# A gated decoder block on one core: the ring of split weights becomes pages, and more of the weight sums are formed by transfers

## The chip, the core and the metric

The kernel runs on one core of a Trainium2 chip. The metric is device time in microseconds (us). TensorE multiplies (PE; its weight loads are listed apart as PEld), VectorE (DVE) and ScalarE (ACT) work on tiles in on-chip memory, GpSimd (POOL) and SyncE (SP) issue transfers here. Transfers from both queues run on the same 16 DMA engines.

## The reference

One decoder block on 256 tokens of width 4096, all in float32:

```
h = rmsnorm(x, norm_w)
u_p, z_p, u_c, b_c, c_c, z_c, g = split(h @ w_in)           # w_in: 4096 x 20480
y_pool = pool(u_p) @ pool_w * pool_scale * silu(z_p)         # trailing means over 2, 4, 8, 16 tokens
y_conv = b_c * conv3(c_c * u_c) * silu(z_c)                  # causal, width 3
br     = [y_pool @ w_branch[0], y_conv @ w_branch[1]]        # 2048 x 4096 each
x      = x + sum(sigmoid(g + gate_b) * br) @ w_out           # 4096 x 4096
out    = rmsnorm(x, final_norm_w)
```

Nearly all the arithmetic is in products of 256 tokens with w_in, w_branch and w_out.

## The kernel before

**Units and steps.** The output columns are cut into 32 units of 1024 columns: convolution units (cu0, cc0, cz0, cb0, cu1, ...), pool units (pz0, pu0, pz1, pu1), gate units (g0_0, g1_0, g0_1, ... g1_3), branch units (b0_0 ... b1_3) and output units (o0 ... o3). A unit runs over its rows in steps of 256 rows. A step loads one raw block of weights (1 MB, 128 partitions x 2 x 1024) into one of three raw buffers.

**Splitting.** A float32 value is multiplied as a high part and a low part. ScalarE writes the high part of a block into the ring (`act`), VectorE writes the remainder, raw minus high (`sub`), and TensorE then multiplies high x high, high x low and low x high, three matmuls of 128 x 512 for each block product.

**Two kinds of step.** A P step makes plain products: 24 matmuls, two VectorE subtractions of 128 x 1024. An S step is one level of a Strassen-like scheme: 21 matmuls instead of 24, but sums of weight blocks are to be formed first. Its raw block has four quarters q0 to q3. Two first sums v = (q0 + q1, q0 + q2) and two last sums (v0 + q2, that + q3) are formed in float32, and then q1, q2, q3, the two v and the two last sums are split. In the code these are `sums` (v into tile V, one VectorE addition of 128 x 1024), `direct` (splits q1 to q3, forms the last sums in tile W), `t13` (splits v) and `t24` (splits W). A table PLACES says which steps of each unit are S steps; there are 207 of them.

**Helped steps.** For some S steps v is not formed by VectorE. SyncE loads q0 twice into a free half of tile E (512 KB), then GpSimd issues a transfer that adds q1 and q2 to it from memory (512 KB). Tile E holds two such halves (`sums_in`, `place_of_sum`); they are free between the end of the last unit's epilogue (`e_done`) and the unit's end. Table HELPED lists which S steps of a unit may be helped, and the rule in `pump` takes one when a half is free and the step's own raw load is at most three loads ahead (LEAD). 53 of the 207 steps are helped.

**The ring.** Split parts lie in a ring of 62 KB a partition, cut into contiguous pieces (`Ring.alloc`): 16 KB for a P step, 28 KB for an S step. Pieces are released in order as matmul groups finish.

**What sets the order.** The program is written out ahead by a planner in Python. `run_step` emits the matmul groups of a step; after every few groups `pump` emits what can be prepared now: a raw load if its buffer has been split (`split`), a sum load, and the splitting of steps up to three ahead, if the ring has room. Every six matmuls `tick` advances a counter `now`, emits one item of the queued epilogue of the unit before, and one item of `fills`. Fills prepare the left operands of the branch and output units: `Fill.fetch` loads 256 KB into a stage (sa, sb or a part of Y), by GpSimd's queue, and ScalarE and VectorE split it into the operand region. All engines then run their lists in order. A raw buffer is released when `direct` has run, so the next load may start while `t13` and `t24` are still to come.

Line numbers of the profile: L69 is `act`, L72 the VectorE helper of all additions and subtractions, L87 SyncE's loads, L91 GpSimd's moves, L94 GpSimd's adding transfers, L1292 the matmul.

Of the kernel before, what the change touches and what calls it, by code (L numbers as in the profile page):

```python
# [32 lines left out]
P = 128  # L33
T = 256
# [11 lines left out]
RING = 62  # L46
# [5 lines left out]
PACE = 5  # L52
TAIL = 3
# [3 lines left out]
def hybrid_block(ctx: ExitStack, tc: tile.TileContext, x, x_t, norm_t, w_first, w_in, pool_w, pool_scale,  # L57
# [48 lines left out]
    ring = sb("ring", [P, RING * KB], F32R)  # L106
# [4 lines left out]
    W = sb("W", [P, 2, NH])  # L111
# [93 lines left out]
    class Ring:  # L205


        def __init__(self, size):
            self.size, self.head, self.live = size, 0, []

        def alloc(self, n):
            at = self.head if self.head + n <= self.size else 0
            for a, m, _, _ in self.live:
                if at < a + m and a < at + n:
                    return None
            if at == 0 and self.head + n > self.size and any(a >= self.head for a, *_ in self.live):
                return None
            block = [at, n, 0, n]
            self.live.append(block)
            self.head = at + n  # L220
            return block

        def release(self, block, n):
            block[2] += n
            while self.live and self.live[0][2]:
                first = self.live[0]
                first[0] += first[2]
                first[1] -= first[2]
                first[2] = 0
                if first[1]:  # L230
                    break
                self.live.pop(0)

    rg = Ring(RING)

    def piece(block, off, n):
        o = (block[0] + off) * KB
        return ring[:, o:o + n * KB]


# [5 lines left out]
    class Step:  # L246
# [7 lines left out]
        def micros(self):  # L254
# [3 lines left out]
            def half(n):  # L258
                def f(block):
                    self.blocks[n] = block  # L260
                    self.h[n] = piece(block, 0, 4).rearrange("p (k n) -> p k n", k=2)
                    self.l[n] = piece(block, 4, 4).rearrange("p (k n) -> p k n", k=2)
                    q = r.rearrange("p (k n) -> p k n", k=2)[:, :, n * NH:(n + 1) * NH]
                    if self is steps[0] and n == 0:

                        act(self.h[n][:, 0], q[:, 0])
                        x_direct(0)
                        for k in range(2):
                            if k:
                                act(self.h[n][:, k], q[:, k])  # L270
                            sub(self.l[n][:, k], q[:, k], self.h[n][:, k].bitcast(F32))
                        return
                    if self is steps[0]:
                        for k in range(2):
                            act(self.h[n][:, k], q[:, k])
                            sub(self.l[n][:, k], q[:, k], self.h[n][:, k].bitcast(F32))
                        return
                    act(self.h[n], q)
                    sub(self.l[n], q, self.h[n].bitcast(F32))
                return f  # L280

            if self.kind == "P":
                self.blocks, self.h, self.l = [None] * 2, [None] * 2, [None] * 2
                return self.pre + [(8, None, half(0)), (8, None, half(1))] + self.post
            if self.kind == "S":
# [8 lines left out]
                def direct(block):  # L294
                    self.bd = block
                    d = piece(block, 0, 12).rearrange("p (i a n) -> p i a n", i=3, a=2)
                    self.dh, self.dl = d[:, :, 0], d[:, :, 1]
                    act(self.dh, q[:, 1:4])
                    add(W[:, 0], v[:, 0], q[:, 2])
                    sub(self.dl, q[:, 1:4], self.dh.bitcast(F32))  # L300
                    add(W[:, 1], W[:, 0], q[:, 3])
                    self.split = True

                def t13(block):
                    self.b13 = block
                    t = piece(block, 0, 8).rearrange("p (i a n) -> p i a n", i=2, a=2)
                    self.h13, self.l13 = t[:, :, 0], t[:, :, 1]
                    act(self.h13, v)
                    sub(self.l13, v, self.h13.bitcast(F32))
                    self.summed = True  # L310

                def t24(block):
                    self.b24 = block
                    t = piece(block, 0, 8).rearrange("p (i a n) -> p i a n", i=2, a=2)
                    self.h24, self.l24 = t[:, :, 0], t[:, :, 1]
                    act(self.h24, W)
                    sub(self.l24, W, self.h24.bitcast(F32))

                return self.pre + self.post + ([] if helped else [(0, None, sums)]) + [(12, lambda: not helped or self.added, direct), (8, None, t13), (8, None, t24)]
            if self.kind == "B":  # L320
                def parts(block):
                    self.block = block
                    self.h = piece(block, 0, 8).rearrange("p (t n) -> p t n", t=2)
                    self.l = piece(block, 8, 8).rearrange("p (t n) -> p t n", t=2)
                    act(self.h, R)
                    sub(self.l, R, self.h.bitcast(F32))

                return [(16, lambda: self.unit.flags.get("base"), parts)]
            if self.kind == "M":
                g = self.g  # L330
                e = E.rearrange("p a n -> p (a n)")[:, g * 1024:(g + 1) * 1024].rearrange(
                    "p (k t) -> p k t", k=4)

                def weights(block):
                    self.bw = block
                    self.h = piece(block, 0, 8).rearrange("p (k n) -> p k n", k=4)
                    self.l = piece(block, 8, 8).rearrange("p (k n) -> p k n", k=4)
                    q = r.rearrange("p (k n) -> p k n", k=4)
                    act(self.h, q)
                    sub(self.l, q, self.h.bitcast(F32))  # L340

                def pooled(block):
                    self.ba = block
                    self.ah = piece(block, 0, 4).rearrange("p (k t) -> p k t", k=4)
                    self.al = piece(block, 4, 4).rearrange("p (k t) -> p k t", k=4)
                    act(self.ah, e)
                    sub(self.al, e, self.ah.bitcast(F32))

                return [(16, None, weights), (8, lambda: self.unit.flags.get(f"pooled{g}"), pooled)]

        def groups(self):

            gs = []
            if self in steps[0:2]:

                for n in range(2):
# [3 lines left out]
                    for i, k in order:  # L360
                        for t in range(2):
                            ah, al = self.op.standing(k, t)
                            h, l = self.h[n][:, k], self.l[n][:, k]
                            gs.append([("E", t, n), [((ah, h), (al, h), (ah, l))[i]], None])
                    gs[-1][2] = [(self.blocks[n], 8)]
            elif self.kind == "P":
                order = [(t, n) for n in self.halves for t in self.toks]
                if self.ending or self.opening:
                    order = [(t, n) for t in self.toks for n in self.halves]
                for t, n in order:  # L370
                    mm = []
                    for k in range(2):
                        ah, al = self.op.standing(k, t)
                        h, l = self.h[n][:, k], self.l[n][:, k]
                        mm += [(ah, h), (ah, l), (al, h)]
                    gs.append([("E", t, n), mm, None])
                    if self.final and t == self.toks[-1]:
                        gs[-1][2] = [(self.blocks[n], 8)]
            elif self.kind == "S":
                prods = {"M1": (A11, self.dh, self.dl, 0, ("F", 0, 0)),  # L380
                         "N3": (Q3, self.dh, self.dl, 1, ("E", 0, 0)),
                         "M2": (A12, self.dh, self.dl, 2, ("E", 0, 1)),
# [1202 lines left out]
```

## Time and profile before

| | before |
|---|---|
| median of 3 runs | 2375.21 us (2372.78 to 2377.42) |
| span of the profiled execution | 2371.9 us |
| granted TensorE clock over the span | 0.999 |
| moved by DMA | 605.60 MB, mean 255 GB/s |

The profile gives no time of the profiled execution beside its span, which runs from the first to the last instruction; the span lies 3.3 us below the median of the runs and 0.9 us below the fastest, so some 1 to 5 us of a run lie around it. An engine's busy time is the union of its instructions; matmuls overlap each other, so the 390 ns of one matmul is longer than the time from one to the next.

### The profile page before, as it was taken

Reading aid. Unit: us, or ns where it says so; the run is one execution under the profiler, and the core shown is the slowest. Engines: PE = TensorE matmul, PEld = TensorE weight load, DVE = VectorE, ACT = ScalarE, POOL = GpSimd, SP = SyncE. Lnnn points to the kernel's source line nnn. Section 1 sums busy time; section 2 is a strip of 40 time slices with the busy share of each in tenths; the row PEclk is TensorE's granted clock in tenths of the full one; section 3 lists DMA queues with packets and bytes.
Section 4 is the critical chain, followed back from the end, with each engine's and each line's share of the span. In section 5 each row is a group of like instructions: output and inputs, shape, how many; then the busy total and the mean of one; then the engine's idle time right before and its main releaser. Section 6 shows DMA issues by size and latency. Waiting matters only on the chain.

```text
span 2371.9 us, 28071 instructions
## 1 busy us (share of the span) xinstructions
PE 2353.5 (99%) x10483; PEld 1946.2 (82%) x10483; DVE 2176.7 (92%) x2234; ACT 1419.7 (60%) x1474; POOL 134.5 (6%) x201
## 2 busy tenths in 40 slices
PE   9999999999999999999999999999999999999998
PEld 7888888888888888888888888887878888878886
DVE  8999899989999989989999999988998898899898
ACT  7565565656555656566665656565664556566564
POOL 0000000000002001000000000001100001000000
PEclk9999999999999999999999999999999999999999
DMA  8578678886778658658887888789866667778867
GB/s 335 189 253 252 224 263 276 261 253 215 262 252 265 224 211 251 231 219 262 278 281 232 295 285 276 244 285 293 285 240 226 260 229 267 244 241 285 280 222 267
DMA packets 105257, 605.60 MB, mean 255 GB/s; under 512 B 11232, under 2 KB 11488, under 8 KB 43936
## 3 DMA queue, kind: packets, MB, share of 16 engines
q1 hardware_dynamic: 83216, 512.30, 59.5%
q0 software_dynamic: 21472, 90.45, 16.0%
q8 instruction: 82, 1.34, 0.2%
q10 hardware_dynamic: 432, 1.07, 0.1%
q14 instruction: 55, 0.45, 0.1%
HBM read 571.26 MB, written 25.17 MB: 251 GB/s over the span
## 4 chain that ended last, share of the span: by engine, by line
PE 90%; DVE 5%; DMA 2%; issue 2%; ACT 1%; SPq 0%; POOL 0%; DVEq 0%; ACTq 0%; POOLq 0%
PE sums L1292 66%; PE shared L1292 22%; DVE ring L72 2%; PE shared L804 1%; PE shared L528 1%; DVE W L72 1%; ACT ring L69 1%; DMA R<-in_gate_b_dram 1%; DMA E<-in_w_in_dram 1%; DVE R L72 0%; DMA raw<-in_w_in_dram 0%; DVE V L72 0%; DVE arena L72 0%; DMA raw<-in_w_out_dram 0%; DVE sa L72 0%
## 5 line engine op out<-in xcount | busy, mean ns | idle before, releaser
L1292 PE MATMUL sums<-ring,arena 128*128 128x512 f32 x7641 | 1806.5, 390 | 2.8 <-ACT E L69 2.4
L1292 PEld LDWEIGHTS sums<-ring,arena 128*128 128x128 f32 x7641 | 1431.6, 188 | 301.1 <-ACT E L69 3.3
L72 DVE TENSOR_TENSOR ring<-raw,ring 128x1024 fp32r<-128x1024 f32 (+2 forms) x695 | 942.4, 1382 | 101.8 <-ACT ring L69 97.7
L69 ACT ACTIVATE ring<-raw 128x1024 fp32r<-128x1024 f32 (+2 forms) x695 | 801.8, 1182 | 284.9 <-PE sums L1292 174.9
L1292 PE MATMUL shared<-ring,arena 128*128 128x512 f32 x2484 | 627.7, 389 | 3.6 <-DVE ring L72 3.6
L1292 PEld LDWEIGHTS shared<-ring,arena 128*128 128x128 f32 x2484 | 465.5, 188 | 102.9 <-DVE ring L72 6.0
L69 ACT ACTIVATE ring<-W 128x1024 fp32r<-128x1024 f32 x207 | 219.9, 1062 | 364.2 <-DVE W L72 302.9
L72 DVE TENSOR_TENSOR ring<-W,ring 128x1024 fp32r<-128x1024 f32 x207 | 253.9, 1226 | 23.1 <-ACT ring L69 11.8
L69 ACT ACTIVATE ring<-V 128x1024 fp32r<-128x1024 f32 x154 | 162.7, 1057 | 144.5 <-DVE V L72 119.9
L72 DVE TENSOR_TENSOR V<-raw 128x1024 f32<-128x1024 f32 x154 | 187.9, 1220 | 7.6 <-DMA raw<-in_w_in_dram 6.8
L72 DVE TENSOR_TENSOR ring<-V,ring 128x1024 fp32r<-128x1024 f32 x154 | 187.9, 1220 | 1.3 <-ACT ring L69 1.3
L72 DVE TENSOR_TENSOR W<-W,raw 128x512 f32<-128x512 f32 x207 | 141.9, 685 | 0.0
L72 DVE TENSOR_TENSOR W<-V,raw 128x512 f32<-128x512 f32 x154 | 106.6, 692 | 4.7
L94 POOL DMA_DIRECT2D E<-in_w_in_dram x47 | 41.1, 875 | 765.1 <-DMA E<-in_w_in_dram 322.7
L72 DVE TENSOR_TENSOR R<-R,E 128x1024 f32<-128x1024 f32 (+1 forms) x49 | 77.1, 1592 | 4.0 <-DMA R<-in_gate_b_dram 1.8
L72 DVE TENSOR_TENSOR ring<-E,ring 128x1024 fp32r<-128x1024 f32 x57 | 69.5, 1219 | 1.9 <-ACT ring L69 1.9
L69 ACT ACTIVATE ring<-E 128x1024 fp32r<-128x1024 f32 x57 | 59.7, 1047 | 6.7 <-PE sums L1292 3.7
L72 DVE TENSOR_TENSOR R<-R,shared 128x512 f32<-128x512 f32 x87 | 59.6, 685 | 2.7 <-ACT R L69 0.8
L69 ACT ACTIVATE arena<-sa 128x512 fp32r<-128x512 f32 (+2 forms) x48 | 25.2, 555 | 57.5 <-DVE sa L72 57.5
L69 ACT ACTIVATE E<-sums,rin 128x512 f32<-128x512 f32 x76 | 49.2, 682 | 15.7 <-PE sums L1292 15.7
L72 DVE TENSOR_TENSOR W<-E,raw 128x512 f32<-128x512 f32 x53 | 36.6, 691 | 12.8 <-issue 5.7
L72 DVE TENSOR_TENSOR arena<-sa,arena 128x512 fp32r<-128x512 f32 (+2 forms) x48 | 27.5, 600 | 3.5 <-ACT arena L69 3.5
(143 smaller groups left out, 560.0 us busy)
## 6 DMA issues: line engine op xcount, KB each, us to landing
raw<-in_w_in_dram SPq DMA_DIRECT2D x318, 1024.0 KB, 5.5
raw<-in_w_branch_dram SPq DMA_DIRECT2D x64, 1024.0 KB, 5.2
raw<-in_w_out_dram SPq DMA_DIRECT2D x64, 1024.0 KB, 5.9
E<-in_w_in_dram SPq DMA_DIRECT2D x47, 512.0 KB, 7.3
E<-in_w_in_dram POOLq DMA_DIRECT2D x47, 512.0 KB, 8.6
gates_d<-R POOLq DMA_DIRECT2D x8, 1024.0 KB, 12.0
R<-in_gate_b_dram POOLq DMA_DIRECT2D x7, 1024.0 KB, 12.0
R<-E POOLq DMA_DIRECT2D x4, 1024.0 KB, 9.4
```

What stands on the lines that cost most here:

```text
L69: return pin(nc.scalar.activation(dst, src, func, **kw))
L72: return pin(nc.vector.tensor_tensor(out=dst, in0=a, in1=b, op=op))
L94: return pin(nc.gpsimd.dma_start(dst, src, accum_op=ALU.add))
L528: pin(nc.tensor.transpose(shared(j)[:, i * T + t * P:i * T + (t + 1) * P], src[:, t, c:c + P], ident))
L804: pin(nc.tensor.matmul(o, a[:, k, ts], b[:, k], start=(k, i) == (0, 0), stop=(k, i) == (3, 2)))
L1292: pin(nc.tensor.matmul(ps, lhs, rhs, start=n == 0, stop=n == u.total[b] - 1))
```

## The change

The matrix products, the PLACES table and the operands stay. What changes:

- The ring becomes 16 pages of 4 KB a partition, a high and a low block of 512 columns in each. A step takes 4 (P) or 7 (S) pages, in any state of the ring; a page is released as soon as its own product is done. P steps therefore run one 128-row half after the other, in groups of three matmuls (six before). Where a block of pages wraps round the ring's end, its `act` and its `sub` become two instructions each.
- Tile W is gone. The last sums are written over q0 and q1 of the raw buffer, which therefore stays held until `t24`.
- Transfers may form v in halves of E and of R, four places instead of two (`r_done`, RWAIT tell when R is free). HELPED is empty and every S step is a candidate: 104 are helped. The raw load of a helped step leaves out q0 (768 KB instead of 1 MB).
- The operand stages are loaded by SyncE's queue instead of GpSimd's (31 loads of 256 KB).

```diff
-RING = 62
+PAGES = 16
...
+RWAIT = 10
...
-    W = sb("W", [P, 2, NH])
...
         def alloc(self, n):
...
+            block = [(self.head + i) % self.pages for i in range(n)]
+            if any(self.used[i] for i in block):
                 return None
...
+        def release(self, *pages):
+            for i in pages:
+                self.used[i] = False
...
+    def split_act(block, src):
+        for i, m, d in parts_of(block):
+            act(d[:, :, 0], src[:, i:i + m])
...
                 def direct(block):
                     self.bd = block
-                    d = piece(block, 0, 12).rearrange("p (i a n) -> p i a n", i=3, a=2)
-                    self.dh, self.dl = d[:, :, 0], d[:, :, 1]
-                    act(self.dh, q[:, 1:4])
-                    add(W[:, 0], v[:, 0], q[:, 2])
-                    sub(self.dl, q[:, 1:4], self.dh.bitcast(F32))
-                    add(W[:, 1], W[:, 0], q[:, 3])
-                    self.split = True
+                    split_act(block, q[:, 1:4])
+                    add(q[:, 0], v[:, 0], q[:, 2])
+                    split_sub(block, q[:, 1:4])
+                    add(q[:, 1], q[:, 0], q[:, 3])
...
                 def t24(block):
                     self.b24 = block
...
+                    split_act(block, q[:, 0:2])
+                    split_sub(block, q[:, 0:2])
+                    self.split = True
...
-                order = [(t, n) for n in self.halves for t in self.toks]
+                order = [(t, n, (k,)) for n in self.halves for k in range(2) for t in self.toks]
...
+    HELPED = {}
...
         def fetch(self, st):
             self.at, self.st = now[0], st
-            move(flat(st), self.src)
+            load(flat(st), self.src)
...
+        elif s.slot is not None:
+            load(r[:, NH:4 * NH], s.src.rearrange("p k n -> p (k n)")[:, NH:4 * NH])
...
-                at = next((i for i in t.slots if sums_in[i] is None or sums_in[i].summed), None)
+                at = next((i for i in t.slots if sums_from[i // 2] is not None and now[0] >= sums_from[i // 2]
+                           and (sums_in[i] is None or sums_in[i].summed)), None)
...
-            t.slots = (0, 1)[:1 + (i < s_at[-1])] if t.kind == "S" else ()
-    sums_in = [None] * 2
+            t.slots = (0, 2, 1, 3)[:4 if i < s_at[-1] else 1] if t.kind == "S" else ()
+    sums_in = [None] * 4
```

The first place is SyncE's list in a gate unit (the five units from g0_1 to g0_3 have the same pattern). A row of `raw` is a weight block, a row of `E` or `R` the first half of a sum that GpSimd's transfer then completes. Before, one unit reads:

```order
L87 DMA E<-in_w_in_dram 128x2x512
L87 DMA raw<-in_w_in_dram 128x2048 x2
L87 DMA E<-in_w_in_dram 128x2x512
L87 DMA raw<-in_w_in_dram 128x2048 x4
L87 DMA E<-in_w_in_dram 128x2x512
L87 DMA raw<-in_w_in_dram 128x2048 x10
```

The same stretch of SyncE's list now:

```order
L88 DMA E<-in_w_in_dram 128x2x512
L88 DMA raw<-in_w_in_dram 128x2048
L88 DMA E<-in_w_in_dram 128x2x512
L88 DMA raw<-in_w_in_dram 128x1536 x2
L88 DMA raw<-in_w_in_dram 128x2048
L88 DMA E<-in_w_in_dram 128x2x512
L88 DMA raw<-in_w_in_dram 128x1536
L88 DMA E<-in_w_in_dram 128x2x512
L88 DMA raw<-in_w_in_dram 128x2048
L88 DMA raw<-in_w_in_dram 128x1536
L88 DMA R<-in_w_in_dram 128x2x512
L88 DMA E<-in_w_in_dram 128x2x512
```

Six sum loads stand in a unit instead of three, one of them into R, and four of the six stand one or two weight loads behind the one before.

The second place is VectorE's list in the same kind of unit, three prepared steps in a row. `W<-E,raw` (before) and `raw<-E,raw` (now) is the addition in `direct` that first reads a sum; `ring<-E,ring` is `t13`, which frees the half of E. Before:

```order
L72 TENSOR_TENSOR W<-E,raw 128x512
L72 TENSOR_TENSOR ring<-raw,ring 128x3x512
L72 TENSOR_TENSOR W<-W,raw 128x512
L72 TENSOR_TENSOR ring<-E,ring 128x2x512
L72 TENSOR_TENSOR ring<-W,ring 128x2x512
L72 TENSOR_TENSOR ring<-raw,ring 128x1024 x2
L72 TENSOR_TENSOR V<-raw 128x1024
L72 TENSOR_TENSOR W<-V,raw 128x512
L72 TENSOR_TENSOR ring<-raw,ring 128x3x512
L72 TENSOR_TENSOR W<-W,raw 128x512
L72 TENSOR_TENSOR ring<-V,ring 128x2x512
L72 TENSOR_TENSOR ring<-W,ring 128x2x512
```

Now, in such a unit, from the addition of one helped step to that of the third helped step, which uses the same half of E:

```order
L73 TENSOR_TENSOR raw<-E,raw 128x512
L73 TENSOR_TENSOR ring<-raw,ring 128x3x512
L73 TENSOR_TENSOR raw<-raw 128x512
L73 TENSOR_TENSOR ring<-E,ring 128x2x512
L73 TENSOR_TENSOR ring<-raw,ring 128x512 x2
L73 TENSOR_TENSOR raw<-E,raw 128x512
L73 TENSOR_TENSOR ring<-raw,ring 128x3x512
L73 TENSOR_TENSOR raw<-raw 128x512
L73 TENSOR_TENSOR ring<-E,ring 128x2x512
L73 TENSOR_TENSOR ring<-raw,ring 128x2x512 x3
L73 TENSOR_TENSOR raw<-E,raw 128x512
```

The `V<-raw` rows are gone here, `ring<-raw,ring 128x512 x2` is a block that wraps round the ring's end, and between the row that frees the half (the fourth) and the row that reads the next sum in it (the last) stand nine VectorE instructions.

More of the change, by code (lines that the diff above doesn't have):

```diff
@@ L313, in t24 @@
                     self.b24 = block
[L314 to L319, printed above, removed]
+                    split_act(block, q[:, 0:2])
+                    split_sub(block, q[:, 0:2])
+                    self.split = True
+                return self.pre + self.post + ([] if helped else [(0, None, sums)]) + [(3, lambda: not helped or self.added, direct), (2, None, t13), (2, None, t24)]
             if self.kind == "B":
@@ L478, in f, with r_done @@
             sums_from[0] = now[0] + n
+        return f
+    def r_done(n=2):
+        def f():
+            sums_from[1] = now[0] + n
         return f
@@ L1426, in unpark @@
         load(parked[c], o_d[c])
-    sums_from[0], running[0] = None, last
+    sums_from[:], running[0] = (None, None), last
     lead = last.steps[:-TAIL]
```

205 lines of the change are left out of this document (92 added, 113 removed).

## The prediction

> **What bounds the kernel now.** I read the page first, then busy time by stage, then the chain, then the places where TensorE stands.
>
> ```profile
> span 2371.9 us, 28071 instructions
> PE 2353.5 (99%) x10483; PEld 1946.2 (82%) x10483; DVE 2176.7 (92%) x2234; ACT 1419.7 (60%) x1474; POOL 134.5 (6%) x201
> ```
>
> TensorE is busy for all but 18.4 us, VectorE for all but 195 us. Busy time of TensorE is modelled, so the pace has to be looked at. One piece of the chain in a gate unit, and the stages (start and end; then busy us of PE, PEld, DVE, ACT, POOL; granted clock, DMA share, GB/s):
>
> ```profile
> 1370.90 6.12 PE sums L1292 x27
> ...
> 900.00:1000.00 100.00, 99.76 (x441) 82.23 (x440) 97.19 (x98) 58.35 (x55) 11.84 (x16) 1.00 0.72 238
> 1300.00:1400.00 100.00, 100.00 (x443) 82.78 (x442) 95.92 (x90) 65.40 (x61) 5.84 (x7) 1.00 0.90 299
> 1600.00:1700.00 100.00, 97.91 (x429) 79.71 (x428) 88.73 (x102) 60.38 (x67) 13.34 (x20) 1.00 0.88 288
> 1700.00:1800.00 100.00, 97.92 (x441) 80.92 (x440) 88.65 (x92) 55.31 (x62) 4.73 (x8) 1.00 0.67 241
> 2000.00:2100.00 100.00, 98.18 (x439) 80.43 (x438) 83.83 (x119) 55.38 (x70) 6.95 (x11) 1.00 0.75 247
> 2100.00:2200.00 100.00, 100.00 (x443) 82.81 (x442) 97.84 (x92) 64.71 (x67) 5.42 (x7) 1.00 0.79 269
> ```
>
> 27 matmuls take 6.12 us, 0.2267 us each, at full clock. A P step is thus 24 x 0.2267 = 5.44 us, an S step 4.76 us. Between 100 and 2300 us only the four stages above with less than 100 hold idle time of TensorE: 0.24 + 2.09 + 2.08 + 1.82 = 6.23 us. That is all that smoother feeding can win in the body. Start and end keep their steps. The three larger pauses, and one VectorE wait ahead of them:
>
> ```profile
> 1647.17 0.73 PE L1292 MATMUL shared<-ring,arena 128*128 128x512 f32 x2 [1.30 <-DVE ring L72]
> 1728.47 3.70 PE L1292 MATMUL sums<-ring,arena 128*128 128x512 f32 x15 [2.08 <-ACT E L69]
> ...
> 1632.64 0.69 DVE L72 TENSOR_TENSOR W<-E,raw 128x512 f32<-128x512 f32 x1 [5.73 <-issue]
> ```
>
> VectorE waited 5.73 us for a transferred sum in g1_3, and 13 us later TensorE paused 1.30 us for the ring. So TensorE has cover for most of such a wait, not for all of it.
>
> **The change part by part.** Costs of VectorE, ScalarE and the transfers (ns of one behind the busy us; for transfers KB and median us to landing):
>
> ```profile
> L72 DVE TENSOR_TENSOR V<-raw 128x1024 f32<-128x1024 f32 x154 | 187.9, 1220 | 7.6 <-DMA raw<-in_w_in_dram 6.8 <-DMA raw<-in_w_out_dram 0.8
> L72 DVE TENSOR_TENSOR ring<-raw,ring 128x1024 fp32r<-128x1024 f32 x480 | 567.5, 1220 | 76.2 <-ACT ring L69 74.1
> L72 DVE TENSOR_TENSOR ring<-raw,ring 128x1536 fp32r<-128x1536 f32 x207 | 363.2, 1755 | 24.4 <-ACT ring L69 22.5 <-PE sums L1292 0.7
> L72 DVE TENSOR_TENSOR W<-W,raw 128x512 f32<-128x512 f32 x207 | 141.9, 685 | 0.0
> ...
> raw<-in_w_in_dram SPq DMA_DIRECT2D x318, 1024.0 KB, 5.5
> E<-in_w_in_dram SPq DMA_DIRECT2D x47, 512.0 KB, 7.3
> E<-in_w_in_dram POOLq DMA_DIRECT2D x47, 512.0 KB, 8.6
> q1 hardware_dynamic: 83216, 512.30, 59.5%
> q0 software_dynamic: 21472, 90.45, 16.0%
> ```
>
> *First sums.* Helped steps go from 53 to 104, so VectorE loses 51 additions of 1.220 us: -62 us. Blocks that wrap round the ring make 83 more VectorE splits (1198 for 1115 in the order); cutting 1024 columns into two 512s costs 2 x 0.685 - 1.220 = 0.15 us each: +12.5 us. Net -50 us of VectorE, from 92% to 90% of the span. None of it lies on the path: TensorE is at 100% in every gate stage while VectorE is at 96%, so its worth is at most the 6.2 us above.
>
> *Order of matmuls.* Groups of three instead of six change banks more often. S steps already do so, and 27 matmuls of S and P mixed take the 6.12 us above. Cost nothing; below nothing is excluded by the same pace.
>
> *Last sums in the raw buffer.* The number of additions is the same. The buffer is released after `t13` and `t24`, so 2 x 1.220 = 2.4 us of VectorE later. The next load lands in 5.5 us and is needed after two more steps, P and S at least: 2 x 1.220 for the P step, and direct, t13 and t24 of a helped S step, 2 x 0.685 + 1.755 + 2 x 1.220 = 5.6 us, together 8.0 us. Hidden, with 2.5 us left; without that cover a load would cost up to 2.4 us.
>
> *Pages.* Release by product gives room earlier; the wait that this can shorten is ScalarE's on TensorE, of which none ended in a pause of TensorE in the gate units:
>
> ```profile
> ACT ring L69 <- PE sums L1292: 248.8, 169, 6.6
> DVE W L72 <- DMA E<-in_w_in_dram: 1.4, 3, 0.7
> POOL sa L91 <- DVE arena L72: 74.4, 5, 38.2
> ...
> SPq L87 <- DVE ring L72: 1056.1, 257, 12.1
> ```
>
> *More sums in transfers.* This adds a wait. The adding transfer can only start when the first half of the sum has landed, and `direct` on VectorE, with everything queued behind it (splits of later steps, epilogue, operand fills), waits for the second landing. So far that wait was 1.4 us in all by name, plus the 5.73 above. What the pair takes is seen in a gate unit (issue by SyncE, issue by GpSimd, first use, and landing min/median/max of both transfers):
>
> ```profile
> 1393.89 0.38 SPq L87 DMA_DIRECT2D E<-in_w_in_dram  x1
> 1403.26 0.86 POOL L94 DMA_DIRECT2D E<-in_w_in_dram  x1 [16.28 <-DVE ring L72]
> 1412.85 0.69 DVE L72 TENSOR_TENSOR W<-E,raw 128x512 f32<-128x512 f32 x1
> DMA to landing us min/median/max: 4.9/8.9/15.0
> ```
>
> From SyncE's issue to use: 18.96 us, with 9.37 us up to GpSimd's issue and the median landing of 8.9 us behind it: 18.3 us for the pair, hardly earlier than the use. By the page's medians, 7.3 + 8.6 = 15.9 us. In the new order, between freeing a half of E and the use of the next sum in it, VectorE has only 2 x 0.685 + 0.685 + 1.755 + 0.685 + 1.220 + 3 x 1.220 = 9.4 us of work. So VectorE will wait there, 6 to 9 us if it comes early. Does TensorE? When VectorE is as far ahead as the pages allow, TensorE still has two steps in hand as the half is freed; then come the freed step and two more before the waiting one: S, P, S, S, P = 111 matmuls = 25.2 us. Against it: 18.3 us, then the addition and the split (0.685 + 1.755), 1.2 us until the half is free: 21.9 us. TensorE keeps 3.3 us. That is hidden, but closely; if VectorE lags by more than 3.3 us at that point, TensorE pays the excess. Counted in VectorE's order, 15 sums away from a unit's start have 10.4 us or less of VectorE work ahead of them.
>
> Here the Trainium skill gives another price: by "DMA: Bandwidth & Descriptors", section "Anatomy of one DMA — SWDGE (gpsimd) path", a transfer takes about 2.0 us plus its bytes at 436 GB/s, an estimate of 3.2 us for 512 KB and 6.4 us for the pair. By that no sum could be late. The trace differs (7.3 and 8.6 us), and the trace decides.
>
> *Bytes.* By the queue rows SyncE's queue takes 0.595 x 2371.9 / 512.3 = 2.75 us of the engines for a MB, GpSimd's 0.160 x 2371.9 / 90.45 = 4.2. A sum is 0.524 MB on each: 3.64 us. A quarter not loaded saves 0.72. So 51 x 3.64 - 104 x 0.72 = +111 us of DMA, 4.7% of the span; in a gate unit of 81 us 3 x 3.64 - 6 x 0.72 = +6.6 us, which lifts its share by 8 points, from 0.90 at 1300 to 0.98. No stage sets its pace by DMA now, but landings will rather lengthen.
>
> *Stage loads on SyncE.* 31 loads move. Behind them on SyncE are raw loads. SyncE already waits for VectorE before nearly each load (1056 us for one line), and the stage is freed by VectorE work emitted just before, so a stage load seldom waits longer than the raw load behind it would. Taken as 0; GpSimd's waits of up to 38.2 us were time in which it had nothing to do. Bounds: a gain of the share of pauses in 1600 to 1800 (4.2 us), a loss of 1 us for each of 12 loads that wait for a fresh store: 12 us.
>
> *Sum.* Of the 6.2 us of pauses, those at 900 and 2000 to 2100 go with the lighter VectorE (-2.1 us). The one behind the late sum in g1_3 stays and doubles, since g1_3 now has six sums for three and three of them with short distances (+1.8 us). Together -0.3 us: 2371.6 for the span, 2375 for the median, which lies 3.3 us above the span. No change, where 0.2% or 4.75 us is what a measurement can tell from none.
>
> **The rivals.**
>
> *The lighter VectorE closes the pauses.* For it: 50 us less work, earlier pages. Against it: the pause at 1728 is behind ScalarE. All 6.2 us gone: 2369, faster by 0.26%.
>
> *Late sums stop TensorE.* For it: the 3.3 us margin. If landings lengthen by the DMA share, 18.3 x 0.98 / 0.90 = 19.9 us, 1.7 us are left, and a lag of VectorE of 3.3 us, as after a unit's epilogue, makes a pause of 1.6 us. It decides from a pair of 20 us with such a lag on. 15 x 1.6 = 24 us: 2399. Against it: VectorE falls from 96% to some 92% in these units, which pays back one wait in each.
>
> *DMA becomes the bound in the gate units.* 0.98 is above every stage shown; if some 0.96 is what can be kept, 2% of six units of 81 us is 10 us: 2385.
>
> *SyncE is held by stage loads.* The 12 us above: 2387.
>
> *VectorE is the true bound.* TensorE at the pace of its own loads would leave the 50 us of VectorE as gain: 2325. Against it: 0.2267 us a matmul whether VectorE is at 84% or 98%. The Trainium skill's "Perfetto Trace Analysis", section "Identifying the Most-Contended Engine", has such a reading: weight-load busy, not matmul busy, tells TensorE's headroom, and PEld is at 82%. By that rule the engine at 92% should be relieved first. The constant pace and the pauses speak against it here.
>
> **How the numbers follow.** No change 0.40 (2371 to 2380 by itself), pauses closed 0.18, late sums 0.25, DMA 0.08, SyncE 0.07, VectorE bound 0.02. Faster 0.18 + 0.02 = 0.20, same 0.40, slower 0.40. The predicted time is 2375. The range reaches down to 2368, past the closed pauses, and up to 2402, past the priced late sums; the tail of the late sums and the last rival lie outside.
>
> **What would show it.** Right: PE at 100% in the gate stages, 0.2267 us a matmul, VectorE some 50 us less busy, waits of VectorE and ScalarE on sums in E and R of 4 to 9 us each at a dozen places or more, DMA share over 0.9 in the gate units. Wrong: pauses of TensorE behind `ring` in the g units (late sums), raw landings well over 5.5 us with SyncE waiting for DMA (bytes), SyncE idle behind sa or sb (stage loads), or a span shorter by more than 6 us.

## The result and the profile after

| | before | after |
|---|---|---|
| median of 4 runs | 2375.72 us (2372.78 to 2377.42) | 2502.75 us (2497.65 to 2508.11) |
| span of the profiled execution | 2371.9 us | 2506.4 us |
| granted TensorE clock over the span | 0.999 | 0.983 |

The changed kernel is slower: 1.0538 of the time before, 95% interval 1.052 to 1.0557, 127 us by the medians. The forecast of 2375 us and its range up to 2402 both missed.

The page of the changed kernel (span, then busy us, share and instructions of each engine):

```profile
span 2506.4 us, 28215 instructions
PE 2398.5 (96%) x10483; PEld 1959.5 (78%) x10483; DVE 2132.4 (85%) x2266; ACT 1418.6 (57%) x1557; POOL 156.8 (6%) x221
```

Three of its stages (start and end; then busy us of PE, PEld, DVE, ACT, POOL; granted clock, DMA share, GB/s):

```profile
1300.00:1400.00 100.00, 90.67 (x379) 74.06 (x380) 82.04 (x78) 55.66 (x55) 7.83 (x9) 0.92 0.84 249
1600.00:1700.00 100.00, 91.54 (x394) 74.71 (x393) 79.72 (x78) 56.43 (x60) 6.98 (x8) 0.97 0.84 257
2100.00:2200.00 100.00, 100.00 (x451) 82.96 (x450) 83.28 (x109) 58.18 (x76) 4.25 (x6) 1.00 0.79 272
```

The 134.5 us between the two spans split in two. TensorE stands idle 2506.4 - 2398.5 = 107.9 us for 18.4 before: +89.5 us. And it is busy 45.0 us longer for the same 10483 matmuls. The five stages from 1200 to 1700 us, mostly gate units and at 98 to 100% before, are at 87 to 95% now, at a granted clock of 0.92 to 0.97. VectorE has 44 us less to do, near the 50 forecast, and nothing was gained by it.

The waits (engine, what it was about to write, what it waited for: us in total, times, longest):

```profile
DVE raw L73 <- DMA E<-in_w_in_dram: 134.3, 29, 10.4
ACT ring L70 <- DMA raw<-in_w_in_dram: 106.3, 59, 8.3
ACT ring L70 <- DMA E<-in_w_in_dram: 93.3, 24, 9.8
PE shared L1291 <- DVE ring L73: 56.0, 25, 7.6
DVE raw L73 <- DMA E<-in_w_branch_dram: 29.4, 3, 11.0
DVE raw L73 <- DMA R<-in_w_in_dram: 20.5, 6, 4.6
```

The first row was 1.4 us, 3 times, for the same sums in tile W. VectorE's longest wait on a sum from w_in is 10.4 us (11.0 on one from w_branch), TensorE's longest behind VectorE 7.6 us. ScalarE's waits for raw blocks, 24.9 us (20 times) before, are the second row now. The transfers (KB each, median us to landing):

```profile
raw<-in_w_in_dram SPq DMA_DIRECT2D x89, 768.0 KB, 8.6
E<-in_w_in_dram SPq DMA_DIRECT2D x67, 512.0 KB, 7.4
E<-in_w_in_dram POOLq DMA_DIRECT2D x67, 512.0 KB, 9.7
R<-in_w_in_dram SPq DMA_DIRECT2D x22, 512.0 KB, 10.6
R<-in_w_in_dram POOLq DMA_DIRECT2D x22, 512.0 KB, 9.7
```

One late sum, from the timeline (start us, us, engine, line, what; in brackets the idle time before it): SyncE's load at 1368.95, GpSimd's adding transfer, the use on VectorE at 1390.16, and TensorE before and after its pause. The row at 1372.00 is the use of the sum before it.

```profile
1368.95 0.38 SPq L88 DMA_DIRECT2D E<-in_w_in_dram  x1
1370.08 1.52 PE L1291 MATMUL sums<-ring,arena 128*128 128x512 f32 x6
1372.00 0.69 DVE L73 TENSOR_TENSOR raw<-E,raw 128x512 f32<-128x512 f32 x1 [1.78 <-DMA E<-in_w_in_dram]
...
1378.43 0.86 POOL L95 DMA_DIRECT2D E<-in_w_in_dram  x1 [14.05 <-DMA E<-in_w_in_dram]
1384.54 0.39 PE L1291 MATMUL shared<-ring,arena 128*128 128x512 f32 x1
1390.16 0.69 DVE L73 TENSOR_TENSOR raw<-E,raw 128x512 f32<-128x512 f32 x1 [10.37 <-DMA E<-in_w_in_dram]
1392.58 1.22 PE L1291 MATMUL shared<-ring,arena 128*128 128x512 f32 x2 [7.65 <-DVE ring L73]
1393.60 2.76 PE L1291 MATMUL sums<-ring,arena 128*128 128x512 f32 x6
```

The half of E is free at 1368.95. The sum is usable 21.2 us later, the first split block 23.6 us later (1392.58). TensorE ran out of work after 16.0 us (1384.93): 7.65 us of pause. Behind it comes what the prediction did not price: six matmuls take 2.76 us and not 1.52. In the trace 135 matmuls start 0.40 to 0.70 us after the one before, most of them 0.43 (the pace is 0.227). Of these 119 stand just behind 13 of TensorE's pauses, and they make 25 of the 45 us of longer busy time; the other 20 us are not followed up here.

### The profile page after: what moved, and what is told of

It is laid out like the page before. It is cut to its first block, busy times and chain, and to the rows that moved or that the text cites. A ratio compares the mean times of both kernels' runs of the same rounds, so it can differ in the third digit from the quotient of the medians.

```text
span 2506.4 us, 28215 instructions
## 1 busy us (share of the span) xinstructions
PE 2398.5 (96%) x10483; PEld 1959.5 (78%) x10483; DVE 2132.4 (85%) x2266; ACT 1418.6 (57%) x1557; POOL 156.8 (6%) x221
## 4 chain that ended last, share of the span: by engine, by line
PE 16%; DMA 16%; DVE 14%; ACT 3%; issue 2%; SPq 0%; ACTq 0%; DVEq 0%; POOLq 0%
PE sums L1291 12%; DVE ring L73 8%; DMA E<-in_w_in_dram 7%; PE shared L1291 3%; DVE R L73 3%; DMA raw<-in_w_in_dram 3%; DVE raw L73 2%; ACT ring L70 2%; DMA E<-in_w_out_dram 2%; DMA E<-in_w_branch_dram 1%; DMA raw<-in_w_out_dram 1%; DMA R<-in_w_in_dram 1%; DVE V L73 1%; DMA raw<-in_w_branch_dram 1%; DMA sb<-y_d 0%
## 5 line engine op out<-in xcount | busy, mean ns | idle before, releaser
L70 ACT ACTIVATE ring<-raw 128x1024 fp32r<-128x1024 f32 (+2 forms) x968 | 1006.7, 1087 | 608.4 <-DVE raw L73 374.3
L73 DVE TENSOR_TENSOR ring<-raw,ring 128x1024 fp32r<-128x1024 f32 (+2 forms) x968 | 1189.1, 1265 | 98.6 <-ACT ring L70 85.9
L70 ACT ACTIVATE ring<-V 128x1024 fp32r<-128x1024 f32 (+1 forms) x111 | 110.0, 997 | 192.0 <-DVE V L73 175.6
L73 DVE TENSOR_TENSOR raw<-E,raw 128x512 f32<-128x512 f32 x80 | 55.3, 692 | 190.9 <-DMA E<-in_w_in_dram 134.3
L70 ACT ACTIVATE ring<-E 128x1024 fp32r<-128x1024 f32 (+1 forms) x92 | 89.0, 976 | 142.5 <-DMA E<-in_w_in_dram 93.3
L73 DVE TENSOR_TENSOR raw<-raw 128x512 f32<-128x512 f32 x207 | 143.1, 692 | 6.2
L73 DVE TENSOR_TENSOR V<-raw 128x1024 f32<-128x1024 f32 x103 | 125.6, 1220 | 9.4 <-DMA raw<-in_w_in_dram 7.9
L73 DVE TENSOR_TENSOR ring<-V,ring 128x1024 fp32r<-128x1024 f32 (+1 forms) x111 | 126.1, 1142 | 0.2 <-ACT ring L70 0.2
L73 DVE TENSOR_TENSOR ring<-E,ring 128x1024 fp32r<-128x1024 f32 (+1 forms) x92 | 102.9, 1126 | 1.7 <-ACT ring L70 1.7
L73 DVE TENSOR_TENSOR raw<-V,raw 128x512 f32<-128x512 f32 x103 | 71.2, 692 | 3.2
L70 ACT ACTIVATE arena<-sa 128x512 fp32r<-128x512 f32 (+2 forms) x48 | 25.2, 556 | 58.8 <-DVE sa L73 58.8
L70 ACT ACTIVATE ring<-R 128x1024 fp32r<-128x1024 f32 (+2 forms) x27 | 29.1, 1080 | 23.6 <-DVE R L73 8.9
```

The lines of the kernel that those rows point to most:

```text
L70: return pin(nc.scalar.activation(dst, src, func, **kw))
L73: return pin(nc.vector.tensor_tensor(out=dst, in0=a, in1=b, op=op))
```

## The experiments

The theory formed on this trace, A: the sum's chain (SyncE's load, landing, GpSimd's adding transfer, landing, VectorE) is longer than the work that TensorE has in hand when the half becomes free. The rivals: the added bytes on the DMA engines, the late release of the raw buffer, the stage loads in SyncE's queue.

**Without the near sums.** LATEST is how many raw loads of notice a sum must have. At 2 there are 54 sums left, all with 16 us or more of VectorE work between issue and use, an estimate that adds up VectorE's instructions in the planner's order; as changed, between a third and two fifths of the 104 have 12 us or less. Pages, late release, halves of R and stage loads all stay.

```diff
-    LATEST = 0
+    LATEST = 2
```

> The changed kernel, but a sum is only taken when its own raw load still stands two loads ahead (LATEST 2 for 0): 54 sums instead of 104, each with 16 us or more of VectorE work between its issue and its use (6 to 24 us in the changed kernel). Late sums: no wait of VectorE on a sum over 2 us, TensorE's pauses in the gate units gone, 2370 to 2385 us. Raw buffers released late: still late after every S step, so most of the loss stays, 2450 us or more. Bytes: about as many as before the change, 2375 to 2400. Stage loads or pages: unchanged, so the pauses between 1700 and 2100 us stay, 2400 or more.

Measured: 2373.1 us, ratio 0.9993 (0.9984 to 1.0003). The whole loss is gone with the sums that were left out, and the other parts of the change, taken together, cost nothing that can be measured. ScalarE's waits for raw blocks are still 73.0 us, 48 times, without a loss. But the edit takes out the near sums and half of the transfers with one stroke; two runs further down, with near sums and no byte more and with the bytes and a shorter chain, tell these apart. The page of this run:

```profile
PE 2353.2 (99%) x10483; PEld 1946.5 (82%) x10483; DVE 2190.0 (92%) x2316; ACT 1423.8 (60%) x1557; POOL 118.6 (5%) x171
```

**Only the nearest left out.** LATEST = 1: 69 sums, by the same estimate 3 of them at most with 12 us or less.

> The changed kernel with LATEST = 1: a sum whose own load is the next one is not made by transfer, which leaves 69 sums instead of 104, 3 of them with 12 us or less of VectorE work between issue and use (39 before this edit). Theory A (only near sums cost): 2375 to 2390 us, within 0.6 per cent of the kernel before. Theory B (the number of transfers, their bytes or the free halves of R cost as such): about 2375 plus 16/51 of the 127 us, 2415 us.

Measured: 2400.2 us, ratio 1.011 (1.0091 to 1.0129), above A's 2390 and below B's 2415. I had put the limit at 12 us; of the 28 sums that are left here with one load of notice most have 15 to 18.5 us by the estimate, so that may not always be enough. The 15 sums more than with LATEST = 2 bring their bytes too, and ScalarE's waits for raw blocks are 107.3 us for 73.0, so this run alone doesn't name the cause. No wait on a sum is long:

```profile
PE shared L1291 <- DVE ring L73: 12.7, 13, 2.0
DVE raw L73 <- DMA E<-in_w_in_dram: 14.4, 9, 2.7
```

**No sum by transfer.**

```diff
-            if k in HELPED.get(u.name, ALL):
+            if k in HELPED.get(u.name, ()):
```

> The changed kernel with no sum made by transfer: VectorE makes all of them, at 104 x 1.22 us = 127 us more than in the changed kernel, 2132 + 127 = 2260 us busy. It shows what the sums by transfer are worth at all. Theory A (TensorE bounds the kernel as long as nothing stops it, and VectorE has room up to some 2260 us): 2372 to 2395 us, so better than with all 104 sums. Theory B (VectorE, with no sum taken off it, becomes the bound in the gate units, where it is the busiest): 2420 us or more.

Measured: 2402.86 us, ratio 1.0121 (1.0106 to 1.0136), above A's 2395 by 8 us, though better than with all 104 sums. So the 54 early sums are worth some 30 us: without them VectorE is busy for 94% of the span, and TensorE pauses often and shortly behind it and ScalarE:

```profile
PE sums L1291 <- DVE ring L73: 4.8, 8, 1.1
PE sums L1291 <- ACT E L70: 4.7, 9, 2.6
PE shared L1291 <- DVE ring L73: 4.6, 9, 1.8
```

Over the number of sums the time goes down and up again: 2403 with none, 2373 with 54, 2400 with 69, 2503 with 104.

**The kernel before with its sums made near.** The same 53 sums and bytes, issued one load ahead and not three.

```diff
-    LEAD, WAIT = 3, 1
+    LEAD, WAIT = 1, 1
```

> The kernel before, but a sum is only taken when its own raw load is the very next one (LEAD 1 for 3): again 53 sums and the same bytes, with 12 to 18 us of VectorE work ahead of their use instead of 13 to 28. Late sums: waits of VectorE on sums of 2 to 6 us at 20 places or more, TensorE pauses behind some of them, 2385 to 2430 us. Raw buffers, bytes, pages, stage loads: nothing of them is changed here, 2370 to 2380.

Measured: 2405.81 us, ratio 1.0131 (1.0116 to 1.0146). Nearness alone, with no byte more (605.60 MB in both), makes the same picture, with 13 waits of VectorE, and not 20, of up to 11.0 us in this row. It read 1.4 us, 3 times:

```profile
DVE W L72 <- DMA E<-in_w_in_dram: 60.0, 13, 11.0
```

And the one before TensorE's longest pause on the timeline, half-rate matmuls behind the pause included:

```profile
1510.52 0.69 DVE L72 TENSOR_TENSOR W<-E,raw 128x512 f32<-128x512 f32 x1 [10.81 <-DMA E<-in_w_in_dram]
1512.93 1.22 PE L1292 MATMUL shared<-ring,arena 128*128 128x512 f32 x2 [6.06 <-DVE ring L72]
1513.95 2.76 PE L1292 MATMUL sums<-ring,arena 128*128 128x512 f32 x6
```

**The raw buffer released late, alone.** In the kernel before, `self.split = True` moved from `direct` to `t24`.

> The kernel before, with the raw buffer of an S step released after t24 instead of after direct, and nothing else; the planner then takes 63 sums, 11 of them with 12 us or less ahead of the use. Raw buffers released late: waits of ScalarE on raw loads rise from 40 us to 100 or more, 2440 us or more. Late sums: only the 11 near sums cost, 2380 to 2410 us, with the pauses behind E and not behind raw.

Measured: 2390.01 us, ratio 1.0065 (1.0048 to 1.0082). But the planner then made 63 sums, 11 of them by the estimate with 12 us or less, and its waits for sums grew as well as those for raw blocks (24.9 us, 20 times, before):

```profile
DVE W L72 <- DMA E<-in_w_in_dram: 20.7, 7, 8.7
ACT ring L69 <- DMA raw<-in_w_in_dram: 43.0, 38, 5.2
```

So this run doesn't give the price of the release by itself. The run with LATEST = 2 says more: it releases late throughout, together with the other parts, and loses nothing in all.

**Stage loads on SyncE, alone.** In the kernel before, `move` became `load` in `Fill.fetch`.

> The kernel before with one part of the change alone: the operand stage loads are issued by SyncE and no longer by GpSimd. Theory A (this part is free): 2370 to 2380 us, within 0.3 per cent of the kernel before. Rival D of the prediction (the load waits on SyncE until its stage is free and holds the raw loads behind it): 2385 us or more, with raw waits on VectorE and ScalarE.

Measured: 2372.81 us, ratio 0.9992 (0.9983 to 1.0002). Free.

**Without the second transfer.** `move_add` in `pump` became `pass`.

> The changed kernel without the adding transfer, so that E and R hold the first addend alone (the second addend and its 512 KB a sum are left out); the planner and the notice of the other loads stay. It takes the second half of the chain away: the wait of GpSimd's queue and the second landing, 11.7 of the 21.2 us in the step I followed. Theory A (the chain from SyncE's issue to the use is what TensorE waits for): a chain of about 9 us is covered by 16 us, so nearly all pauses go; 2373 to 2390 us. Theory B (the wait comes from SyncE's queue or from raw blocks that arrive late, not from the second landing): 2440 us or more.

Measured: 2365.45 us, ratio 0.9965 (0.9952 to 0.9978). All of the loss hangs on the second transfer, on its place in the chain or on its bytes. With 104 sums at one landing, no wait of VectorE or ScalarE on a sum is left, and TensorE's largest wait in the trace is 1.1 us.

```profile
PE 2351.1 (99%) x10483; PEld 1947.8 (82%) x10483; DVE 2133.1 (90%) x2266; ACT 1426.9 (60%) x1557; POOL 68.3 (3%) x117
```

Chain and bytes went together here. Three runs were to tell them apart; two failed at it.

**Bytes to an unread tile.** The adding transfer became two halves into one tile `aside`.

> The changed kernel with all 104 sums and all their bytes, but the adding transfer writes to a tile that nobody reads (as two transfers of half the size), so a split waits for the first load alone. Left out: the second addend of the helped first sums. Late sums: the chain to the use falls from about 21 us to about 9, the waits of VectorE on E and R go, 2365 to 2385 us. Bytes: the DMA share and the loss stay, 2450 us or more. Raw buffers released late: the loss stays, 2450 or more.

Measured: 2466.27 us, ratio 1.0399 (1.0371 to 1.0426), by neither theory. The experiment made a wait of its own:

```profile
POOL aside L95 <- DMA aside<-in_w_in_dram: 1085.8, 166, 13.3
SPq L88 <- DMA gates_d<-R: 79.2, 6, 20.3
ACT ring L70 <- DMA raw<-in_w_in_dram: 195.6, 87, 16.5
```

The transfers into one tile wait for each other on GpSimd, the gate's store behind them is late, SyncE's next load into R waits for the store, and the raw loads behind that load are held.

**Bytes to device memory, not waiting.**

```diff
-                move_add(v.rearrange("p i n -> p (i n)"), w)
+                move(aside_d[next(asides)], w)
```

> The changed kernel in which each adding transfer is replaced by a plain transfer of the same 512 KB, at the same place of GpSimd's queue, into a block of device memory that nobody reads; E and R keep the first addend alone (the second addend is left out of the sums). The bytes and the number of transfers stay, the chain ends with the first landing. Theory A (the length of the chain is the cost, not the bytes): as without the second transfer, 2364 to 2380 us. Theory B (the bytes of the second addends slow every landing): 2400 us or more, with the waits for raw and E still there.

Measured: 2447.85 us, ratio 1.0309 (1.0295 to 1.0323), against A as I had put it. With nothing to wait for, GpSimd ran ahead of the rest: eight transfers in the first 6 us, where the kernel starts (timeline), and more as each landed.

```profile
1.53 4.24 POOL L92 DMA_DIRECT2D aside_d<-in_w_in_dram  x8
```

They landed in 14.0 us at the median, and waits for raw blocks took the place of those for sums (waits):

```profile
DVE raw L73 <- DMA raw<-in_w_in_dram: 81.0, 20, 8.4
ACT ring L70 <- DMA raw<-in_w_in_dram: 164.6, 55, 10.1
```

So bytes can cost, if they come at a bad moment; whether they do at the adds' own place was still open.

**Bytes at their place, chain ended.** The second transfer stores the first addend: it waits for the first landing as the add does, and nobody waits for it but the next load into that half.

```diff
-                move_add(v.rearrange("p i n -> p (i n)"), w)
+                move(aside_d[next(asides)], v.rearrange("p i n -> p (i n)"))
```

> The changed kernel in which each adding transfer is replaced by a plain one that stores the first addend, out of the half of E or R into a block of device memory that nobody reads: 512 KB again, and GpSimd waits for the first landing as before, so that these transfers cannot start earlier than the adds did. The second addend is left out of the sums, and the use no longer waits for the second transfer. Theory A (the length of the chain up to the use is the cost): 2365 to 2385 us. Theory B (half a megabyte more at this place slows raw loads and first landings, as the waits for raw blocks in the run with the copies into device memory suggest): 2420 us or more, with waits for raw blocks and first sums on VectorE and ScalarE.

Measured: 2378.7 us, ratio 1.0016 (1.0006 to 1.0025). Of the loss, 124 us are gone with the bytes still there. They cost 13 us beside the run without them, in waits for raw blocks and none of VectorE or ScalarE for sums; the DMA share at TensorE's full pace is 0.87. The waits, and a stage:

```profile
ACT ring L70 <- DMA raw<-in_w_in_dram: 121.2, 70, 8.0
DVE raw L73 <- DMA raw<-in_w_in_dram: 35.8, 23, 5.0
```

```profile
1300.00:1400.00 100.00, 100.00 (x443) 82.78 (x442) 91.43 (x89) 62.80 (x62) 6.09 (x10) 1.00 0.87 299
```

One thing isn't kept. The store moves as many bytes as the add, out to device memory, but keeps the DMA engines busy for less time. GpSimd's queue in the changed kernel, and here:

```profile
q0 software_dynamic: 26336, 109.06, 19.5%
q0 software_dynamic: 26336, 109.06, 14.1%
```

Of their spans, 2506.4 and 2379.0 us, that is 489 and 335 us; the run without the second transfer has 201 (8.5% of 2363.0). By this estimate an add takes 2.8 us of all 16 engines and a store 1.3. So the bytes are cleared as a cause, the time that the adds take of the engines not fully. The next run speaks to that.

**The chain with an eighth of the second bytes.**

```diff
-                move_add(v.rearrange("p i n -> p (i n)"), w)
+                move_add(v[:, :, 0:64], w.rearrange("p (i n) -> p i n", i=2)[:, :, 0:64])
```

> The changed kernel whose adding transfers move the first 64 of 512 columns of each half alone, 64 KB for 512 KB (the second addend is left out for the other columns); GpSimd's wait for the first landing, the issue and the second landing stay in the chain. Theory A with a chain whose second part is mostly the moving of bytes: the second landing falls from about 9 us to 3 or 4 us, the chain to 15 or 16 us, just what the 16 us of cover measured in one step holds, so most pauses go; 2370 to 2400 us. If the second part is mostly fixed cost (issue, start, notice of the landing): 2440 us or more.

Measured: 2426.34 us, ratio 1.0211 (1.0196 to 1.0226), between the two cases. The adding transfer of 64 KB lands in 6.8 us where the one of 512 KB took 9.7:

```profile
E<-in_w_in_dram POOLq DMA_DIRECT2D x67, 64.0 KB, 6.8
R<-in_w_in_dram POOLq DMA_DIRECT2D x22, 64.0 KB, 6.2
```

So some 70% of the landing is left with an eighth of the bytes (in rows of 256 bytes, so part of it may be the price of short rows), and 40% of the loss (51 of 127 us) stays, with VectorE still waiting:

```profile
DVE raw L73 <- DMA E<-in_w_in_dram: 98.5, 19, 9.4
```

GpSimd's queue takes 11.4% of 2425.9 us here, 277 us, less than the stores of the run before, and yet 51 us are lost for 4. For these 51 us the chain is enough as a cause; how the other 76 us divide between the longer landing and the engines' time that the full adds take was not tried.

**The cover, by a lighter VectorE.** Without `add(q[:, 1], q[:, 0], q[:, 3])` in `direct`.

> The changed kernel without the add that makes each S step's last sum, raw<-raw of 128x512: 207 instructions of about 0.69 us, so 143 us less VectorE work; the matmuls that use that sum get the unsummed block, so part of the computation is left out. All 104 sums by transfers, their 3 loads of notice, their bytes and the order of the rest stay. Theory A (the cover is too small because VectorE runs behind the place that its pages allow): VectorE catches up faster after each wait and is nearly always as far ahead as the pages allow, so at a chain of 21 us against 25 us of TensorE work most pauses go; 2375 to 2410 us. Theory B (the pages themselves don't cover the chain, however far ahead VectorE is): the pauses stay, 2460 us or more.

Measured: 2438.91 us, ratio 1.0271 (1.0256 to 1.0287), between A and B.

```profile
DVE raw L73 <- DMA E<-in_w_in_dram: 151.5, 29, 11.1
PE shared L1290 <- DVE ring L73: 32.4, 12, 6.9
```

VectorE waits for the sums as often and as long as before this edit; TensorE pauses behind it 12 times and not 25. So half of the loss goes with VectorE's lag. The other half, 65 us, stays. At the five longest pauses from 1260 to 1630 us VectorE had caught up: just ahead of the step that frees the half, ScalarE waited 1.9 to 2.8 us, for a raw block in three of them and for TensorE to free pages in two. Still TensorE ran out of work 15.9 to 18.8 us after SyncE's issue. The last of them, with ScalarE's wait for pages and, 16.9 us after SyncE's issue at 1600.51, TensorE's pause:

```profile
1596.07 1.49 ACT L70 ACTIVATE ring<-raw 128x1536 fp32r<-128x1536 f32 x1 [1.90 <-PE shared L1290]
1624.28 1.22 PE L1290 MATMUL shared<-ring,arena 128*128 128x512 f32 x2 [6.92 <-DVE ring L73]
```

So raw blocks and pages hold the lead below the predicted cover even where VectorE isn't the limit. Which of them would have to change first was not tried.

**More notice.** LATEST = 2 with LEAD = 4, in search of a version that beats both.

> The changed kernel with LATEST = 2 and LEAD = 4: the same 54 sums as with LATEST = 2 alone, 22 of them issued one load earlier where a half of E or R is free by then. Theory A (sums with 16 us of VectorE work or more between issue and use are covered already): no change against LATEST = 2 alone, 2370 to 2376 us. Rival (part of the last pauses is still a sum that is just late): 2366 to 2369 us, and a version that beats both kernels.

Measured: 2378.75 us, ratio 1.0017 (1.0008 to 1.0026). No gain, rather 4 us of loss. Of the versions with the whole computation none was faster than the kernel before by more than a measurement can tell.

## Why the prediction was wrong

**The step that failed is the cover in "More sums in transfers".** It set 25.2 us of TensorE work, "when VectorE is as far ahead as the pages allow", against a need of 21.9 us and kept a margin of 3.3 us. Both count from the start of `t13`, 1.2 us before the half is free; from there on they are 24.0 and 20.7 us. In the sum followed above the cover was 16.0 us and the need 23.6. The need was off by 2.9 us (chain 21.2 for 18.3), the cover by 8.0. In work: the 25.2 us are 10.2 for two steps in hand and 15.0 for the three steps from the freed one on. Measured from the start of `t13` there were 17.2 us, so about 2 us in hand and not 10.2. At the six longest pauses from 1230 to 1670 us the cover was 14.1 to 17.9 us and the need 19.9 to 23.6. The assumption held the mistake: VectorE is not as far ahead there. It came out of waits for two sums (9.85 us at 1299.27, and the row below) and then worked through to 1363.8 with no wait over 0.3 us, the last unit's epilogue included, without getting its lead back:

```profile
1315.45 0.69 DVE L73 TENSOR_TENSOR raw<-R,raw 128x512 f32<-128x512 f32 x1 [2.96 <-DMA R<-in_w_in_dram]
```

Just ahead of the step that frees the half, ScalarE also waited 0.3 to 1.5 us for a raw block at five of the six pauses. I saw the condition, named it, and gave VectorE 4 points of slack, "which pays back one wait in each". They are taken from the one stage at 96%; over 1200 to 1700 us VectorE was at 92% before (461.95 of 500 us). The run with a VectorE lighter by another 143 us shows that half of the loss stays even then, and that raw blocks and pages, too, keep the lead below 25 us.

**The count of paying sums was too small, and so was the price of each.** "Late sums stop TensorE" was the right rival with the right mechanism, and the trace's pauses behind `ring` in the g units are the sign named for it. It was priced at 15 sums of 1.6 us, 24 us. VectorE waited for sums 41 times (197.8 us), and in five gate units TensorE paused 4.4 to 7.7 us at one place (at 1296, 1385, 1477, 1566 and 1658 us). The limit of 10.4 us of VectorE work was probably too low: with one load of notice next to none of the sums are below it, and 27 us more than with two are lost. In the forecast's own sum the doubled pause of g1_3 stands as +1.8 us, where its row has 1.30; that is too little to matter.

**Not priced at all: the slower matmuls behind a pause,** a part of the +45 us of busy time.

**DMA.** A share of 0.98 was forecast for the gate units; measured were 0.82 to 0.89, at TensorE's slower pace. The price per MB was not too high: by the queue rows both queues together take 157 us more of the engines (77.7% of 2506.4 us for 75.5% of 2371.9), where 111 were forecast. From 1200 to 1700 us the share is 0.84 for 1927 matmuls; an estimate for the 2193 of the kernel before is 0.96. Whether the engines could keep that is open, since no run has all adds at full pace. The stores in the adds' place reach 0.87 and cost 13 us, near the 10 us of the DMA rival, through waits for raw blocks.

**Right, or right within a measurement.** VectorE's work: -50 forecast, -44.3 found. Finer matmul groups and pages: TensorE keeps its pace at 100% in the undisturbed stages, and the run with 54 sums has all of them. The late raw release and SyncE's stage loads at 0: the same run for both together, and the stage loads alone; what the late release adds to the waits for raw blocks beside late sums was not taken apart. The 6.2 us as all that smoother feeding can win: the run without the second transfer, whose TensorE hardly pauses, is 8.2 us faster than the kernel before.

**Left open.** Why the second of two sums that are issued within 4 us of each other is so late. One such in the changed kernel, SyncE's issue and GpSimd's:

```profile
1348.08 0.77 SPq L88 DMA_DIRECT2D E<-in_w_in_dram  x1
1362.52 0.85 POOL L95 DMA_DIRECT2D E<-in_w_in_dram  x1 [10.85 <-DMA E<-in_w_in_dram]
```

14.4 us lie between them. A raw block, the gate's 1 MB and the other sum's add are under way at that time; which of them holds it was not tried.

## What to carry to other kernels

Price a chain of transfers by its landings under load and not by its bytes, and set it against the lead that the consumer has at that place in the trace, not against the most that the buffers allow. A helper that takes work off a busy engine pays while its result is early; a rule for taking it needs a limit of notice, and here a limit of two loads, which leaves half of the sums, took away a loss of 127 us. When an experiment replaces a transfer, keep what it waits for, or it will run ahead and disturb something else.

## What the runs showed of the hardware

Thirteen pauses of TensorE in the changed kernel are followed by matmuls at half rate: six in 2.76 us instead of 1.52. In the trace the granted clock is 0.5 there for 3.4, 6.8 or 10.2 us each time, which gives 0.92 over the stage from 1300 and 0.983 over the span. All nine pauses of 2.8 us or more are among the thirteen, and four of 1.3 to 2.6 us; five others of 1.8 to 2.8 us are not. After the pause of 2.08 us in the kernel before, 15 took 3.70 us, close to the full rate. The Trainium skill has a rule for this in "TensorE: Matmul & The Clock Gate", section "What's actually happening": after an idle window of about 3.4 us the clock is halved until TensorE has been busy for such a window again. The trace agrees in the length of the slow stretches; the four short pauses are not covered by the rule so put. The prediction should have used it: behind the thirteen pauses the slow starts cost 25 us, 2.0 us on top of each.

An adding transfer of 64 KB took 6.8 us and one of 512 KB 9.7, at DMA shares of 0.79 and 0.84 over the gate units. The Trainium skill's fit in "DMA: Bandwidth & Descriptors", section "Anatomy of one DMA — SWDGE (gpsimd) path", would give estimates of 2.2 and 3.2 us. The trace has about three times as much, in the step between them (2.9 us for 1.0) as in the part that is left without the bytes. The fit is for GpSimd's path; the prediction put the sum's first load, by SyncE, at the same price. An add of 512 KB took the engines longer than a plain store of it, by the estimate above 2.8 us for 1.3.
